# A row softmax whose loads and stores all go through one DMA queue, in one fixed order of 4 MB transfers

## Chip, cores, metric

The kernel runs on one core of one Trainium2 chip. Times are microseconds (us) on the device. The kernel before takes 162.96 us (median of 3 runs, 162.91 to 163.17). The profiled span, from first to last instruction, is about 1.8 us shorter than the time (161.2 against 162.96 us here).

## The reference, cut to what matters

```python
def reference(x):                       # x: float32, 16 x 1024 x 512
    x_scaled = x / 0.5
    x_max = np.max(x_scaled, axis=-1, keepdims=True)
    exp_x = np.exp(x_scaled - x_max)
    return exp_x / np.sum(exp_x, axis=-1, keepdims=True)
```

There are 16384 rows of 512 numbers; 33.55 MB are read and 33.55 MB written.

## The kernel before

The rows are split into 8 tiles (C = 8) of 128 partitions x 16 rows x 512, 4 MB each. A tile is worked on in four blocks of 4 rows. DVE (VectorE) takes the maximum and scales three rows of four; ACT (ScalarE) makes the exponentials with their sums and scales the fourth row. Loads are issued from Sync, stores from ACT, so two queues are at work (q1 and q10 in the profile). Six buffers of a whole tile exist.

```python
data = ctx.enter_context(tc.tile_pool(name="data", bufs=6))
...
def load(c):
    xt = tiles[c] = data.tile([P, G, D], fp32, name="xt")
    for lo, hi in FIRST if c == 0 else [(0, G)]:          # FIRST = [(0, 4), (4, 16)]
        nc.sync.dma_start(out=xt[:, lo:hi, :], in_=xr[c][:, lo:hi, :])
...
def store(i):
    c, b = blocks[i]
    if b + B == G:
        nc.scalar.dma_start(out=outr[c], in_=tiles[c])

n = len(blocks)
for i in range(n + 3):
    if i < n:
        if blocks[i][1] == 0:
            load(blocks[i][0])
        shift(i)                    # DVE: maximum, bias
        exponentials(i)             # ACT: 4 exponentials, each with its sum
    if 1 <= i <= n:
        scale_vector(i - 1)         # DVE: reciprocal, 3 scalings
    if 2 <= i <= n + 1:
        scale_scalar(i - 2)         # ACT: 1 scaling
    if 3 <= i:
        store(i - 3)
```

Of the kernel before, what the change touches and what calls it, by code (L numbers as in the profile page):

```python
# [1 line left out]

# [4 lines left out]


@with_exitstack
def kernel(  # L10
    ctx: ExitStack,
    tc: tile.TileContext,
    x: bass.AP,
    out: bass.AP,
):
    nc = tc.nc
    fp32 = mybir.dt.float32
    P = nc.NUM_PARTITIONS
    AX = mybir.AxisListType.X
    EXP = mybir.ActivationFunctionType.Exp  # L20
    COPY = mybir.ActivationFunctionType.Copy
    MAX = mybir.AluOpType.max

    D = x.shape[-1]
    xf = x.flatten_outer_dims()
    of = out.flatten_outer_dims()
    N = xf.shape[0]




    G = 16
    B = 4
    N_ACT = 1
    C = N // (P * G)
    assert C * P * G == N
    xr = xf.rearrange("(c p g) d -> c p g d", p=P, g=G)
    outr = of.rearrange("(c p g) d -> c p g d", p=P, g=G)

    FIRST = [(0, 4), (4, 16)]  # L40

    data = ctx.enter_context(tc.tile_pool(name="data", bufs=6))
    stats = ctx.enter_context(tc.tile_pool(name="stats", bufs=6))

    ctx.enter_context(tc.manual_schedule())


    warm = stats.tile([P, 1], fp32, name="warm", bufs=1)
    nc.vector.memset(warm, 0.0)  # L49
    nc.scalar.activation(out=warm, in_=warm, func=EXP)  # L50

    tiles = {}
    blocks = [(c, b) for c in range(C) for b in range(0, G, B)]
    state = {}

    def load(c):
        xt = tiles[c] = data.tile([P, G, D], fp32, name="xt")
        for lo, hi in FIRST if c == 0 else [(0, G)]:
            nc.sync.dma_start(out=xt[:, lo:hi, :], in_=xr[c][:, lo:hi, :])  # L59

    def shift(i):
        c, b = blocks[i]
        xb = tiles[c][:, b : b + B, :]
        negmax = stats.tile([P, B], fp32, name="negmax")
        nc.vector.tensor_reduce(negmax, xb, axis=AX, op=MAX, negate=True)  # L65
        bias = stats.tile([P, B], fp32, name="bias")
        nc.vector.tensor_scalar_mul(bias, negmax, 2.0)  # L67
        state[i] = (xb, bias)

    def exponentials(i):  # L70
        xb, bias = state[i]
        sums = stats.tile([P, B], fp32, name="sums")
        for g in range(B):
            nc.scalar.activation(  # L74
                out=xb[:, g, :],
                in_=xb[:, g, :],
                func=EXP,
                bias=bias[:, g : g + 1],
                scale=2.0,
                accum_out=sums[:, g : g + 1],  # L80
            )
        state[i] = (xb, sums)

    def scale_vector(i):
        xb, sums = state[i]
        recip = stats.tile([P, B], fp32, name="recip")
        nc.vector.reciprocal(recip, sums)  # L87
        for g in range(B - N_ACT):
            nc.vector.tensor_scalar_mul(xb[:, g, :], xb[:, g, :], recip[:, g : g + 1])  # L89
        state[i] = (xb, recip)  # L90

    def scale_scalar(i):
        xb, recip = state[i]
        for g in range(B - N_ACT, B):
            nc.scalar.activation(  # L95
                out=xb[:, g, :], in_=xb[:, g, :], func=COPY, scale=recip[:, g : g + 1]
            )

    def store(i):
        c, b = blocks[i]  # L100
        if b + B == G:
            nc.scalar.dma_start(out=outr[c], in_=tiles[c])

    n = len(blocks)
    for i in range(n + 3):
        if i < n:
            if blocks[i][1] == 0:
                load(blocks[i][0])
            shift(i)
            exponentials(i)  # L110
        if 1 <= i <= n:
            scale_vector(i - 1)
        if 2 <= i <= n + 1:
            scale_scalar(i - 2)
        if 3 <= i:
            store(i - 3)


# [1 line left out]
_INS = ['x']  # L120
_OUTS = [((16, 1024, 512), 'float32')]


# [23 lines left out]
```

## Time and profile before

| | before |
|---|---|
| span | 161.2 us |
| DVE, ACT busy | 74%, 71% |
| packet time in the two DMA queues, as a share of 16 engines | 49.2% + 48.2% = 97.4% |
| a 32 KB packet (packet records; median in the load, mixed and store phases) | 1213 ns |
| all bytes at that pace on 16 engines | 155.3 us |

Lines of the page of the kernel before. Part 2 has 40 slices of the span: a digit is the busy share in tenths, then come the GB/s. Part 3 has a queue's packets, MB and share of the engines' time; part 5 has a group of instructions with its busy time, the mean ns of one, and the idle time before it with what ended it; part 6 has the issues, with the median time to landing.

```profile
span 161.2 us, 563 instructions
DVE 119.7 (74%) x193; ACT 114.8 (71%) x290; POOL 0.2 (0%) x4
...
DMA  5999999998999999999999999999999999999991
GB/s 193 457 463 447 390 463 447 392 455 317 417 472 398 431 472 398 423 480 398 423 472 409 390 488 423 390 488 423 390 488 423 390 488 425 390 480 431 390 480 65
...
q1 hardware_dynamic: 1296, 33.56, 49.2%
q10 hardware_dynamic: 1152, 33.55, 48.2%
q14 instruction: 4, 0.03, 0.0%
...
L65 DVE TENSOR_REDUCE negmax<-xt 128x4 f32<-128x2048 f32 x32 | 73.0, 2281 | 19.8 <-DMA xt<-in_x_dram 19.8
...
out_dram<-xt ACTq DMA_DIRECT2D x8, 4096.0 KB, 26.9
xt<-in_x_dram SPq DMA_DIRECT2D x7, 4096.0 KB, 47.3
```

The DMA engines are busy in every slice but the first and the last. Their pace is the same in the load, mixed and store phases (1213 ns), and packets fill 97.4% of their time, so the kernel is bound by its bytes; what can still be lost lies at the start, at the end and in single slow packets. While loads and stores are mixed they share the engines evenly: from 40 to 118 us 511 packets of 32 KB start in each queue, and where the packet that follows another on its engine can be told by its start (661 cases), 587 times it is one of the other queue. The four packets of queue 14, 8 KB each, are listed as `instruction`.

Windows of the kernel before (columns: stretch, its length, busy us and count of DVE, ACT, POOL, then PEclk, DMA share, GB/s; a packet is counted where it starts):

```profile
34.00:36.00 2.00, 1.97 (x6) 1.80 (x5) 0.00 (x0) 1.00 0.74 311
36.00:38.00 2.00, 1.97 (x3) 1.75 (x6) 0.00 (x0) 1.00 1.21 360
...
158.00:159.00 1.00, 0.00 (x0) 0.00 (x0) 0.00 (x0) 1.00 0.23 98
159.00:160.00 1.00, 0.00 (x0) 0.00 (x0) 0.00 (x0) 1.00 0.00 0
```

There is a dip after the first store is issued (34.2 us): the load packets just before the first store packets, which start at 38.6 us, are slow (1.5 to 2.1 us, against 1213 ns). The last packets start before 159 us and end at 159.9 us.

### The profile page before, as it was taken

The numbers are of one execution on the slowest core, as the hardware profiler recorded it, in microseconds if no ns is written. First come the engines' busy times: TensorE is split into PE (matmuls) and PEld (weight loads), VectorE is DVE, ScalarE is ACT, GpSimd is POOL, SyncE is SP. The second block draws the span as 40 slices with busy tenths as digits, with TensorE's granted clock in tenths as the row PEclk, the third lists the DMA queues.
The fourth block names the chain that finished last, engine by engine and source line by source line (L and its number), as shares of the span: only waits on it lengthen the run. The fifth ranks groups of instructions, "written<-read, shape, count | busy, mean of one in ns | idle before, by whom it ended". The sixth has DMA issues, their size and how long they took to land.

```text
span 161.2 us, 563 instructions
## 1 busy us (share of the span) xinstructions
DVE 119.7 (74%) x193; ACT 114.8 (71%) x290; POOL 0.2 (0%) x4
## 2 busy tenths in 40 slices
DVE  0608999999999999999994999359991799930000
ACT  3072799999999998999995799809997199980000
POOL 0000000000000000000000000000000000000000
DMA  5999999998999999999999999999999999999991
GB/s 193 457 463 447 390 463 447 392 455 317 417 472 398 431 472 398 423 480 398 423 472 409 390 488 423 390 488 423 390 488 423 390 488 425 390 480 431 390 480 65
DMA packets 2452, 67.14 MB, mean 416 GB/s; under 512 B 272, under 2 KB 272, under 8 KB 272
## 3 DMA queue, kind: packets, MB, share of 16 engines
q1 hardware_dynamic: 1296, 33.56, 49.2%
q10 hardware_dynamic: 1152, 33.55, 48.2%
q14 instruction: 4, 0.03, 0.0%
HBM read 33.55 MB, written 33.55 MB: 416 GB/s over the span
## 4 chain that ended last, share of the span: by engine, by line
DMA 54%; DVE 31%; ACT 3%; issue 1%; SPq 0%
DMA xt<-in_x_dram 36%; DVE negmax L65 19%; DMA out_dram<-xt 18%; DVE xt L89 10%; ACT xt L74 2%; DVE bias L67 1%; ACT xt L95 1%; DVE recip L87 1%; SPq L59 0%
## 5 line engine op out<-in xcount | busy, mean ns | idle before, releaser
L74 ACT ACTIVATE xt<-xt,bias 128x512 f32<-128x512 f32 x128 | 90.8, 710 | 28.9 <-DVE bias L67 28.9
L65 DVE TENSOR_REDUCE negmax<-xt 128x4 f32<-128x2048 f32 x32 | 73.0, 2281 | 19.8 <-DMA xt<-in_x_dram 19.8
L89 DVE TENSOR_SCALAR xt<-xt,recip 128x512 f32<-128x512 f32 x96 | 40.9, 483 | 1.1
L74 ACT ACTIVATION_READ_ACCUMULATOR xt<-xt,bias 128x1 f32 x128 | 23.9, 187 | 0.0
L95 ACT ACTIVATE xt<-xt,recip 128x512 f32<-128x512 f32 x32 | 22.4, 706 | 0.0
L87 DVE RECIPROCAL recip<-sums 128x4 f32<-128x4 f32 x32 | 5.5, 171 | 1.6 <-ACT xt L74 1.6
L67 DVE TENSOR_SCALAR bias<-negmax 128x4 f32<-128x4 f32 x32 | 5.5, 170 | 1.1
L50 ACT ACT_TABLE_LOAD x1 | 1.3, 1283 | 0.7 <-PEq L131 0.7
L49 DVE MEMSET warm<- 128x1 f32 x1 | 0.1, 59 | 0.8 <-PEq L131 0.8
L50 ACT ACTIVATE warm<-warm 128x1 f32<-128x1 f32 x1 | 0.2, 203 | 0.0
L131 POOL MEMSET const-bfloat16-1.0<- 128x1 bf16 x1 | 0.1, 101 | 0.0
L131 POOL MEMSET const-uint8-127<- 128x1 uint8 x1 | 0.1, 101 | 0.0
L131 POOL MEMSET const-float32-0.0<- 128x1 f32 x1 | 0.1, 98 | 0.2 <-issue 0.2
L131 POOL MEMSET const-float32-1.0<- 128x1 f32 x1 | 0.1, 98 | 0.0
## 6 DMA issues: line engine op xcount, KB each, us to landing
out_dram<-xt ACTq DMA_DIRECT2D x8, 4096.0 KB, 26.9
xt<-in_x_dram SPq DMA_DIRECT2D x7, 4096.0 KB, 47.3
xt<-in_x_dram SPq DMA_DIRECT2D x1, 3072.0 KB, 11.5
xt<-in_x_dram SPq DMA_DIRECT2D x1, 1024.0 KB, 4.7
```

Of the source, the lines that this page charges most:

```text
L49: nc.vector.memset(warm, 0.0)
L50: nc.scalar.activation(out=warm, in_=warm, func=EXP)
L65: nc.vector.tensor_reduce(negmax, xb, axis=AX, op=MAX, negate=True)
L67: nc.vector.tensor_scalar_mul(bias, negmax, 2.0)
L74: nc.scalar.activation(out=xb[:, g, :], in_=xb[:, g, :], func=EXP, bias=bias[:, g : g + 1], scale=2.0, accum_out=sums[:, g : g + 1],)
L87: nc.vector.reciprocal(recip, sums)
L89: nc.vector.tensor_scalar_mul(xb[:, g, :], xb[:, g, :], recip[:, g : g + 1])
L95: nc.scalar.activation(out=xb[:, g, :], in_=xb[:, g, :], func=COPY, scale=recip[:, g : g + 1])
L131: nc = _bacc.Bacc("TRN2", target_bir_lowering=False, num_devices=1)
```

## The change

It puts all DMA into one queue with a fixed order: four tiles of loads, then a store and a load in turn. ACT issues no DMA any more, and a store stands one block earlier in the loop. The hope is an orderly stream and an ACT free of queue work.

```diff
-            nc.scalar.dma_start(out=outr[c], in_=tiles[c])
+            nc.sync.dma_start(out=outr[c], in_=tiles[c])
+            if c + 4 < C:
+                load(c + 4)
...
-    for i in range(n + 3):
+    for i in range(n + 2):
         if i < n:
-            if blocks[i][1] == 0:
-                load(blocks[i][0])
+            if i == 0:
+                for c in range(4):
+                    load(c)
...
-        if 3 <= i:
-            store(i - 3)
+        if 2 <= i <= n + 1:
+            store(i - 2)
```

With L for a tile's load and S for its store, the queue holds L0 L1 L2 L3 S0 L4 S1 L5 S2 L6 S3 L7 S4 S5 S6 S7. I call a border from a load to a store a turn: there are five, L3-S0, L4-S1, L5-S2, L6-S3 and L7-S4.

## The prediction

> **What bounds the kernel now.** Traffic. The page counts 67.14 MB, 416 GB/s over a span of 161.2 us; DVE is busy 74%, ACT 71%. Queue shares are 49.2% (loads, Sync) plus 48.2% (stores, ACT) = 97.4% of 16 engines' time. The trace's packet records say why: a 32 KB packet takes 1213 ns (median) in the pure load, the mixed and the pure store phase alike. 16 x 32768 B / 1213 ns = 432 GB/s; all bytes at that pace need 155.3 us. The first packet starts at 1.8 us, so 157.0 us is the earliest end; most packets end by 158.8, the last at 159.9. Above the ideal are about 1.8 us of packet time per engine: the first short packets (about 0.5) and some 35 slow load packets (1.5 to 2.1 us each) at 35-40 us, just after the first store (34.2 us) opens the second queue (about 1.2). The windows view shows this dip: 311 and 360 GB/s at 34-38 us. The chain of waits names DVE early (31%) only because loads run ahead.
>
> **What the change does.** No bytes or arithmetic go. By the order listing, DVE is unchanged, ACT loses 8 stores (0.34 us each of sequencer time, off the path), and Sync has 4 tiles of loads, then S0 L4 S1 L5 S2 L6 S3 L7 S4..S7. Instead of alternating by packet on each engine, loads and stores run in blocks of 4 MB, 9.7 us each. [...]
>
> **Does the one queue run dry?** A tile's compute takes 15.2 us (four blocks of 3.79); the first is ready at 34. Estimate at 9.7 us per tile: L0-L3 end at 40.6, S0 50, L4 60, S1 70, L5 79, S2 89, L6 99, S3 108, L7 118, four stores to 157. Stores are ready at 34, 49, 64, 79.5, 95, 110, 127, 139, against starts at 41, 60, 79, 99, 118, 128, 137, 147: slack at least 7 us. L6 and L7 wait for S0 and S1, which land long before. Tile 7's reduce waits some 4 us for its load, in slack. The store's earlier place in the loop gains nothing: ACT's sequencer runs ahead and already issues early stores within 0.3 us of their last scale.
>
> **Time.** Same bound, same ends (1.8 us start, about 1.3 tail, 1.75 outside the span). If the slow packets at 35-40 us come from the second queue's opening, they go: -1.2 us. The skew at the end may shrink. Against it: nine changes of direction within one queue, whose cost no trace here shows; 0.1 us each would be 0.9. Net about -0.8: 162.2 us, range 160.6 to 164.2. Floor: 157.0 + 1.3 + 1.75 = 160.0, so faster by over 2% (below 159.7) is nearly excluded. Chances: faster 0.03, same 0.92, slower 0.05.
>
> **What would show it.** Right: one queue with over 96% share, 1213 ns packets, no dip at 35-40 us, stores issued at 34, 49, 64, 79; DVE's waits for loads below the present 19.8 us; last load landing near 119 instead of 125.8 us, the end about the same. Wrong: holes in GB/s at each load-store border, or a slow stretch also with one queue (then mixing directions costs, not the second queue).
>
> **What would make it wrong.** A bubble of 0.5 us or more at each border; a limit on outstanding work in one queue that delays issues; engines drifting apart in one ring.

The sum: 162.96 - 0.8 = 162.2 us. The 0.1 us for a change of direction was assumed; as the text says, no trace showed one.

## The result

The changed kernel takes 165.16 us (165.05 to 165.25, 4 runs), against 163.06 us for the kernel before (162.91 to 163.21, 4 runs). The ratio is 1.0128 with a 95% interval of 1.0111 to 1.0146. The change costs 2.1 us, and the time lies outside the predicted range of 160.6 to 164.2.

The same lines of the page of the changed kernel:

```profile
span 163.3 us, 566 instructions
DVE 119.6 (73%) x193; ACT 114.8 (70%) x290; POOL 0.2 (0%) x4
...
DMA  5999899999799999989989999999999999999970
GB/s 183 459 466 433 385 506 393 403 490 385 323 441 401 482 401 417 474 385 449 449 385 484 409 417 466 401 433 457 393 457 433 409 474 395 433 466 393 457 321 32
...
q1 hardware_dynamic: 2448, 67.11, 96.5%
q14 instruction: 4, 0.03, 0.0%
...
L65 DVE TENSOR_REDUCE negmax<-xt 128x4 f32<-128x2048 f32 x32 | 72.9, 2279 | 17.6 <-DMA xt<-in_x_dram 17.6
...
out_dram<-xt SPq DMA_DIRECT2D x8, 4096.0 KB, 27.1
xt<-in_x_dram SPq DMA_DIRECT2D x7, 4096.0 KB, 34.3
```

The queue never ran dry, and the stores were issued when I had said. From the timeline (start, duration, queue, line, what):

```profile
34.11 0.35 SPq L102 DMA_DIRECT2D out_dram<-xt  x1
...
49.27 0.34 SPq L102 DMA_DIRECT2D out_dram<-xt  x1
...
64.43 0.34 SPq L102 DMA_DIRECT2D out_dram<-xt  x1
```

The windows of the changed kernel show two things that I had not said:

```profile
38.00:40.00 2.00, 1.97 (x6) 1.88 (x5) 0.00 (x0) 1.00 0.88 279
40.00:42.00 2.00, 1.93 (x4) 1.75 (x6) 0.00 (x0) 1.00 0.94 246
...
158.00:159.00 1.00, 0.00 (x0) 0.00 (x0) 0.00 (x0) 1.00 0.16 66
159.00:160.00 1.00, 0.00 (x0) 0.00 (x0) 0.00 (x0) 1.00 0.15 66
160.00:161.00 1.00, 0.00 (x0) 0.00 (x0) 0.00 (x0) 1.00 0.15 66
161.00:162.00 1.00, 0.00 (x0) 0.00 (x0) 0.00 (x0) 1.00 0.00 0
```

First, the dip did not go with the second queue; it moved with the first store packets and again lies just before them (the slow load packets start at 38.7 to 40.7 us, and the median engine ends these loads at 42.5 us). Second, from 158 to 161 us the DMA share is 0.15: two packets of 1213 ns over 16 engines' 1 us is 0.15. Two engines were still at work while fourteen had finished.

Why two engines are enough to set the time, the packet records show. Every transfer of these two kernels ends with 16 packets of 4 bytes (272 for 17 transfers), a transfer of one partition with a single one (late_one below: its four loads add eight packets, and four of these are under 512 B). So I take each as the end of one engine's part. The end of the changed kernel agrees: its last two 32 KB packets start at 160.60 and 160.83 us, and 1.21 us later, at 161.82 and 162.04 us, the last two 4-byte packets start; the other 14 of this store had ended by 158.9. What waited for a transfer waited for the last of its 16: tile 7's first maximum starts at 123.44 us, 0.3 us after the last one of L7 and 3.4 us after the median one (before: at 125.80, 0.4 us after the last and 2.6 us after the median). And the span ends 1.3 us after the last one of S7 in both kernels. The times of the 4-byte packets give each engine's lateness. The table has the time at which the median engine ended a transfer, and how far the last two engines were behind it (us, worked out from the packet records of the two profiles). While the two queues of the kernel before are mixed, lateness in one queue is not the lateness of the engine (in few_two below it is 1.7 us in the load queue at L3 and 0.3 us in the store queue at S0); the rows S7 can be compared.

```
changed kernel                              before, load queue
transfer  median   2nd last  last           transfer  median   2nd last  last
L2         31.57   0.14      0.57           L2         31.45   0.21      0.26
L3         42.48   0.20      1.47           L3         45.77   0.69      1.87
S0         52.16   0.86      1.47
L4         61.89   1.38      2.32           L4         65.13   0.69      1.87
S1         71.57   1.39      2.32
L5         81.25   1.86      2.32           L5         84.52   1.37      2.17
S2         90.93   1.86      2.76
L6        100.66   2.63      3.07           L6        103.88   1.49      2.17
S3        110.34   2.63      3.07
L7        120.02   2.63      3.07           L7        123.24   1.49      2.17
                                            before, store queue
S7        158.82   3.00      3.22           S7        158.34   1.49      1.60
```

So the 2.1 us are accounted for: the median engine ends 0.5 us later (158.82 against 158.34), and the last engine is 1.6 us further behind it (3.22 against 1.60).

The table also shows when it happens. The instruction packets of the changed kernel start at 31.8, 43.9, 88.4 and 134.8 us, last 309 ns each, and are followed by a gap or slow packet on the engine that carried one; an engine falls 0.4 to 0.7 us behind by one. Those are the steps at L2 (0.57), S0 (0.86), S2 (2.76) and after L7. All other steps, 0.3 to 0.9 us each, stand at L3, L4, L5 and L6: at the turns. None stands at S1 or S3, where a store is followed by a load, and none at L7, the fifth turn. For one of the two engines the sum is 1.3 us by two fetches and 1.8 us by turns; for the other 0.9 and 2.1. The slow packet at one of these turns is among the late engine's last three of the load (at L4 one of them runs from 60.90 to 63.01 us). It begins between 1.5 us before and 0.2 us after the median engine ends its loads, and runs on while others store.

Theory A, then: an engine that has been put out of step, first by an instruction fetch, loses more at the turns of a one-queue order in large blocks; with loads and stores mixed by packet it does so less. Rivals: B, one queue for both directions costs by itself; C, two engines are slow by their place; D, fetches cost only their own bytes, and turns add nothing.

### The profile page after: what moved, and what is told of

It reads as the page before. It is cut to its first block, busy times and chain, and to the rows that moved or that the text cites. A ratio compares the mean times of both kernels' runs of the same rounds, so it can differ in the third digit from the quotient of the medians.

```text
span 163.3 us, 566 instructions
## 1 busy us (share of the span) xinstructions
DVE 119.6 (73%) x193; ACT 114.8 (70%) x290; POOL 0.2 (0%) x4
## 3 DMA queue, kind: packets, MB, share of 16 engines
q1 hardware_dynamic: 2448, 67.11, 96.5%
## 4 chain that ended last, share of the span: by engine, by line
DVE 47%; DMA 34%; ACT 5%; issue 1%; SPq 0%; ACTq 0%
DMA xt<-in_x_dram 34%; DVE negmax L65 28%; DVE xt L89 15%; ACT xt L74 4%; DVE bias L67 2%; ACT xt L95 1%; DVE recip L87 1%; ACTq L145 0%; SPq L59 0%; SPq L102 0%
## 5 line engine op out<-in xcount | busy, mean ns | idle before, releaser
L65 DVE TENSOR_REDUCE negmax<-xt 128x4 f32<-128x2048 f32 x32 | 72.9, 2279 | 17.6 <-DMA xt<-in_x_dram 17.6
```

The source lines that it names most:

```text
L65: nc.vector.tensor_reduce(negmax, xb, axis=AX, op=MAX, negate=True)
```

## The experiments

Experiments with wrong numbers move the same bytes in the same transfers. Lateness is always the last engine's end behind the median engine's, in the profiled run, so it stands for one execution of each kernel. Every ratio is to the kernel before in the same rounds.

### Fewer turns: six_ahead, pairs

six_ahead loads six tiles ahead, then a store and a load in turn (`range(4)` and `c + 4` become `range(6)` and `c + 6`). pairs does

```diff
-                for c in range(4):
+                for c in range(6):
                     load(c)
...
-            if c + 4 < C:
-                load(c + 4)
+            if c == 1:
+                load(6)
+                load(7)
```

> The changed kernel with six tiles of loads ahead in its one queue instead of four: the turns from loads to stores fall from four (L3-S0, L4-S1, L5-S2, L6-S3, L7-S4 are five with the last) to three. Theory A (two of the 16 DMA engines fall behind, first by an instruction fetch, then more at each turn from loads to stores): the two late engines end 2.0 to 2.7 us after the median engine, not 3.0 to 3.2, and the span is 162.3 to 162.9 us against 163.3. Rival B (one queue for both directions costs by itself, wherever the turns are): lag and span as in the changed kernel, 163.3 within 0.2.

> One queue, six tiles ahead, then two stores, two loads, six stores: only two turns from loads to stores. Theory A: late engines end 1.6 to 2.2 us after the median, span 161.6 to 162.4 us. Rival B: span 163.3 within 0.2.

six_ahead: 170.59 us (ratio 1.0448), a mistake of mine. There are six buffers, so L6 waits until S0 has landed, and Sync holds S1 behind that wait (L6 and L7 waited for stores for 61.2 us in all): the queue ran dry, and later once more (3.2 and 2.0 us of idle time per engine in the packet records). Its windows:

```profile
70.00:72.00 2.00, 2.00 (x1) 2.00 (x6) 0.00 (x0) 1.00 0.42 180
72.00:74.00 2.00, 1.93 (x7) 1.75 (x6) 0.00 (x0) 1.00 0.00 0
...
104.00:106.00 2.00, 2.00 (x2) 2.00 (x7) 0.00 (x0) 1.00 1.30 524
106.00:108.00 2.00, 1.93 (x7) 1.75 (x6) 0.00 (x0) 1.00 1.09 262
```

It does not test the number of turns, but it showed two things. After a dry stretch the engines are in step again (lateness 1.71 before, 0.30 after). And the next turn after it costs every engine about 1 us again (1.0 us of excess packet time per engine around 83 us, 1.1 around 106), like the first turn of each run, while the second to fifth turns of the changed kernel cost the median engine nothing.

pairs: 163.79 us (ratio 1.0035, 1.0010 to 1.0059), span 162.2, lateness 2.16. Same queue, same bytes, four instruction packets as in the changed kernel, right numbers, two turns in place of five, and 1.4 us faster than the changed kernel. This lies in theory A's range and outside B's.

### More turns: halves

```diff
-            nc.sync.dma_start(out=outr[c], in_=tiles[c])
-            if c + 4 < C:
-                load(c + 4)
+            ...
+            for lo in (0, G // 2):     # store and load half a tile in turn
+                nc.sync.dma_start(out=outr[c][:, lo:hi, :], in_=tiles[c][:, lo:hi, :])
+                if c + 4 < C:
+                    nc.sync.dma_start(out=xt[:, lo:hi, :], in_=xr[c + 4][:, lo:hi, :])
```

> The changed kernel with stores and loads alternating by half tiles (2 MB, packets of 16 KB): nine turns from loads to stores instead of five, same bytes. Theory A: late engines end 4 us or more after the median, span 164.3 or more. Rival B: span 163.3 within 0.3. If packets of 16 KB cost something themselves, the median engine ends later too, which would be read apart.

166.32 us (ratio 1.0187), span 164.0. The median engine ended 0.5 us later than in the changed kernel (159.32), but the lateness was 3.31, not 4 or more. Theory A in its simple form, so much for each turn, fails here: turns closer together, with packets of 16 KB, cost less each (3.31 us after nine of them, 3.22 after five in the changed kernel). The lateness seems to be bounded.

### Without fetches, and one engine late on purpose: few_one, quiet_one, late_one

few_one uses one activation for a block and one scaling on DVE in place of three, and drops the bias product (wrong numbers); quiet_one also makes blocks of 8 rows (the first load is cut at 8 rows too), scales on DVE alone and stores as soon as a tile is done. The queue's order stays.

```diff
-        for g in range(B):
-            nc.scalar.activation(out=xb[:, g, :], in_=xb[:, g, :], func=EXP,
-                bias=bias[:, g : g + 1], scale=2.0, accum_out=sums[:, g : g + 1])
+        nc.scalar.activation(out=xb, in_=xb, func=EXP,
+            bias=bias[:, 0:1], scale=1.0, accum_out=sums)
```

late_one is quiet_one plus, after the first block's exponentials,

```diff
+                for k in range(4):     # [1, 2047]: one engine, 8 KB; never read
+                    nc.scalar.dma_start(out=late[k : k + 1, 0:2047], in_=...)
```

> The changed kernel's queue and order, with one activation per block instead of four, one scaling instead of three, and no bias product: wrong numbers on purpose, same bytes, so few instructions that none should have to be fetched in the run. Theory A: no instruction packets inside the run, no engine out of step, the last engine ends within 0.6 us of the median, span 159.9 to 160.6 us. Rival C (two engines are slow by their place, whatever is fetched): they still end 2 us or more after the median, span 162 or more. Rival B: span 163 or more.

> The one queue in the order of the changed kernel, with blocks of 8 rows, one instruction each for maximum, exponential and scaling (wrong numbers on purpose, same bytes and the same transfers): so few instructions that nothing should be fetched before the last stores. Theory A (an engine put out of step by a fetch loses more at each turn from loads to stores): without a fetch no engine lags over 0.6 us at the end, last store's median engine at 158.8, span 159.9 to 160.7 us. Rival C (two engines slow by their place): a lag of 1.5 us or more remains, span over 161.3.

> The one-queue kernel with few instructions, plus four loads of one partition (8 KB each, one engine) into an unused tile in the first microseconds, which put one engine some 1.3 us out of step before the first turn. Theory A: this one engine loses more at the turns, ends 2.2 us or more behind the median, and the span is 161.6 us or more. Rival D (only the fetched bytes delay, turns add nothing): it ends 1.2 to 1.5 us behind, span about 161.1.

few_one: 163.18 us, runs from 162.59 to 163.27 (ratio 0.9989). The fetches were halved, not gone (`q14 instruction: 2` on its page, at 63 and 68 us); lateness 1.48, span 161.5. That is half way, in theory A's direction, outside its range; B's and C's numbers for the lateness or the span did not come either.

quiet_one: 162.96 us (ratio 0.9980), span 160.9, no instruction packet in the run. Lateness 1.18, above the 0.6 that I had expected, but no fetch was needed for it: one engine 0.3 us behind after the first turn grew to 0.44, 0.77 and 1.18 at L5, L6 and L7.

late_one: 165.08 us (ratio 1.0112), span 163.2. Four loads, 33 KB out of 67 MB, on one engine, cost 2.1 us against quiet_one. Windows of quiet_one, then of late_one:

```profile
157.00:158.00 1.00, 0.00 (x0) 0.00 (x0) 0.00 (x0) 1.00 1.14 492
158.00:159.00 1.00, 0.00 (x0) 0.00 (x0) 0.00 (x0) 1.00 0.08 33
159.00:160.00 1.00, 0.00 (x0) 0.00 (x0) 0.00 (x0) 1.00 0.00 0
```

```profile
158.00:159.00 1.00, 0.00 (x0) 0.00 (x0) 0.00 (x0) 1.00 0.08 33
159.00:160.00 1.00, 0.00 (x0) 0.00 (x0) 0.00 (x0) 1.00 0.08 33
160.00:161.00 1.00, 0.00 (x0) 0.00 (x0) 0.00 (x0) 1.00 0.08 33
161.00:162.00 1.00, 0.00 (x0) 0.00 (x0) 0.00 (x0) 1.00 0.00 0
```

A share of 0.08 is one packet of 1213 ns in 16 us: one engine alone. Its lateness, from the packet records:

```
            L2    L3    S0    L4    S1    L5    S2    L6    S3    L7    S7
quiet_one  0.19  0.30  0.30  0.35  0.35  0.44  0.44  0.77  0.77  1.18  1.18
late_one   1.08  1.89  1.90  2.73  2.73  2.73  2.73  3.14  3.14  3.40  3.40
later_one  2.40  3.24  3.24  3.24  3.24  3.24  3.24  3.80  3.80  3.80  3.80
```

After L2 every step of late_one stands at a load that precedes a store. Rival D is out: the engine was given 1.08 us of lateness and lost 2.3 us more. Rival C is out as the whole cause, because this engine was chosen by me; but in quiet_one an engine lost 1.0 us that was given nothing, and why it was that engine no run shows.

### Two queues with few instructions: quiet_two, late_two, few_two

The same reductions in the kernel before.

> The two queues of the kernel before, with the same few instructions (wrong numbers on purpose). Theory A: no fetch, so the late engines of the kernel before (1.5 to 1.6 us behind the median at its end) go too: lag under 0.6 us, span 159.4 to 160.2 us; the difference between one queue and two shrinks from 2.1 us to under 0.7. Rival C: lag and difference stay.

> The same four one-engine loads in the two-queue kernel with few instructions. Theory A: loads and stores mix by packet and there is only one turn, so the engine ends 1.2 to 1.7 us behind the median, and the one-queue kernel with the same loads ends at least 0.7 us later than this one. Rival D: both end equally late within 0.5 us.

> The kernel before, two queues, with one activation, one scaling and no bias product for each block of four rows (wrong numbers on purpose), so half the instruction fetches. Theory A: the last engine, 1.6 us behind the median in the kernel before, is at most 1.0 us behind, span 160.2 to 160.9 us. If an engine falls far behind in the mixed phase as in quiet_two, span over 162, and then mixing by packet is not safe by itself.

quiet_two: 169.44 us (ratio 1.0379). With nothing fetched, one engine fell behind all the same, by 1.5 us at L3 and 8.8 us at L6 in the load queue (6.4 us at S3 in the store queue), all during the mixed phase; tiles then came so late that the stores ran dry at about 139 us. late_two: 164.68, 164.69, 168.01 and 171.08 us, two of them over 1.5% above the fastest; in the profiled run (164.68) the last store was issued only at 149.4 us, and the queue had run dry. Blocks of 8 rows make the last tile too late for two queues, where its load lands after 128 us. Neither run can be compared with its one-queue partner. But quiet_two shows that mixing by packet is no protection by itself; why that engine went on losing while those of the kernel before kept their lateness for 19 us of mixing (1.87 in the load queue at L3 and at L4) stays open.

few_two (blocks of 4 rows, few instructions): 162.03 us (ratio 0.9927, 0.9911 to 0.9944), span 160.3, lateness 0.74, as theory A said. The median engine ended its last store at 158.34 us, as in the kernel before, so the gain lies in the lateness: the kernel before, too, seems to carry its fetches to the end. The fewer instructions also move the first store forward, which this run does not part from the fetches.

### More fetches: pool_one, pool_two

```diff
+    for _ in range(512):
+        nc.gpsimd.memset(busy[0:1, :], 0.0)       # GpSimd is idle otherwise
```

> The changed kernel, right numbers, plus 512 one-element memsets on the otherwise idle GpSimd, which touch nothing of the work but whose instructions have to be fetched, some four times 8 KB, most of it before the first turn. Theory A: the engine that carries GpSimd's fetches is put some 2 us or more out of step before the first turn, loses more at the turns, ends 4 us or more behind the median; span 164.3 us or more against 163.3. Rival D (fetches only cost their own bytes, the turns cost the two known engines by their place): the third engine ends at most 2.7 us behind, span stays at 163.3 within 0.3.

> The same idle memsets in the kernel before, two queues. Theory A as first stated (one turn only, then mixing): the lateness stays near the fetched amount, 2 to 3 us behind the median at the end, span 161.4 to 162.8 us, so that the one-queue kernel with memsets is at least 1.8 us slower than this one. But the run with two queues and few instructions had one engine fall 8 us behind in the mixed phase: if being out of step costs there as well, this span is over 163.

pool_one: 165.18 us (ratio 1.0115), span 163.5. Eight fetches instead of four; three engines late in place of two, by 2.29, 2.90 and 3.53 us. The third late engine came with the added fetches. But I had expected 4 us or more and a span of 164.3; the lateness stayed below 3.6, and the span is the one that D had. pool_two: 163.88 us (ratio 1.0036), span 162.0 and lateness 2.51, as said. The two differ by 1.3 us and not by 1.8. The direction holds, and again the lateness in one queue is bounded.

### Is the dip the first store's or the turn's: early_two, early_one

```diff
+            if c == 0 and lo == 0:      # 64 KB of zeros, overwritten later by S0
+                nc.sync.dma_start(out=outr[0][:, 0, 0:128], in_=first)    # scalar in early_two
```

> The kernel before, plus a store of 64 KB of zeros to rows that the first tile's store overwrites later, issued with the first loads. If the slow load packets at 35 to 40 us (about 1 us on every engine) are a cost of the very first store of a run, they go, and the span falls by 0.6 to 1.0 us to about 160.4. If they belong to the turn of full-rate loads to stores (the run with six tiles ahead showed about 1 us at each turn that followed a dry queue), nothing goes: 161.0 to 161.6.

> The same early store in the changed kernel's one queue, between the first two loads. First-store theory: the slow packets at 38 to 42 us go, span 162.1 to 162.7 us. Turn theory: they stay, span 163.1 to 163.7.

early_two: 163.12 us (ratio 0.9990), span 161.6. early_one: 165.45 us (ratio 1.0118), span 163.7. The excess packet time at the turn fell from 1.0 to 0.6 us per engine and from 1.2 to 0.8, but did not go, and neither span fell. The dip belongs mostly to the turn, and six_ahead says the same.

### Does the queue or the order cost: mix_one, mix_cols

Both keep the one queue and alternate small pieces in it; mix_one by 16 partitions, mix_cols by two rows of all 128 partitions.

```diff
+                for lo in range(0, G, 2):                     # mix_cols
+                    hi = lo + 2
+                    nc.sync.dma_start(out=outr[c][:, lo:hi, :], in_=tiles[c][:, lo:hi, :])
+                    nc.sync.dma_start(out=xt[:, lo:hi, :], in_=xr[c + 4][:, lo:hi, :])
```

> The changed kernel with its one queue, but stores and loads of the mixed part cut into pieces of 16 partitions (one packet for each engine) and issued in turn, so that loads and stores alternate by packet as with two queues, right numbers. If the blocks of 4 MB cost (theory A), the last engine ends at most 2.2 us behind the median, near the 1.6 of the kernel before, and the two late engines do not jump at 60, 80 and 100 us. If one queue costs (rival B), the lag stays at 3 us or more. Small transfers may move the median engine later by themselves (about 0.04 us for each extra transfer in the run with halves, so up to 2 us), hence the verdict is on the lag behind the median, not on the time.

> The changed kernel, right numbers, with stores and loads of the mixed part cut into pieces of two rows of all 128 partitions (0.5 MB, 1.2 us of each engine) and issued in turn in the one queue. Theory A: as with two queues, no jumps of the late engines at 60, 80 and 100 us, last engine at most 2.2 us behind the median. Rival B: 3 us or more behind. The many transfers may move the median itself by up to 2 us; the verdict is on the lag. If alternating in one queue is slow by itself, the packets will be over their pace (1213 ns for 32 KB), as in mix_one.

mix_one failed as an experiment: 205 to 251 us, four runs that do not agree. In the profiled one (250.53 us) a 32 KB packet took 2.57 us on average in the mixed part (80 to 200 us) instead of 1.21. It says nothing of queue or order.

mix_cols: 165.47 us (ratio 1.0139), right numbers. Its packets of 4 KB took 159 ns against 152 at the pace of 32 KB packets, and the median engine ended at 160.67 us, 1.9 us later than in the changed kernel. The lateness is 1.73 us at the end, about that of the kernel before (1.60), and from 42 to 120 us the last engine's value never grew: 1.03 at the first piece, 1.00 at the last but one. Only with the last piece of load, where the pure stores begin and an instruction packet falls (121.6 us), it rose by 0.7. It had five instruction packets where the changed kernel has four. Its windows at the times of the former turns:

```profile
60.00:62.00 2.00, 1.93 (x6) 1.75 (x5) 0.00 (x0) 1.00 1.03 420
80.00:82.00 2.00, 2.00 (x4) 2.00 (x7) 0.00 (x0) 1.00 1.03 422
100.00:102.00 2.00, 2.00 (x2) 2.00 (x7) 0.00 (x0) 1.00 1.02 416
```

One queue with a fine mix did not build up the lateness (1.03 us to 1.00); one queue with blocks of 2 or 4 MB did (3.31 us in halves, 3.22 in the changed kernel). Rival B is out as far as the lateness goes. That mix_cols is not faster is the price of its small transfers: in its mixed part the median engine took 1.25 us for each 0.5 MB piece instead of 1.21. It changes the packet size (4 KB for 32 KB) along with the mix, and no run parts these two.

### How the loss depends on turns and lateness: late_pairs, later_one

late_pairs is late_one in the order of pairs; later_one has eight one-engine loads for four.

> The kernel with few instructions and one engine put late on purpose (wrong numbers on purpose), in the order of six tiles of loads, two stores, two loads, six stores: two turns where the run late_one had five. Theory A: that engine starts from 1.1 us, gains 0.7 to 0.9 at each of two turns and ends 2.4 to 2.9 us behind, not 3.4, with the span 0.5 to 1.0 us below the 163.2 of late_one. Rival B: 3.4 and 163.2.

> As late_one with eight one-engine loads instead of four, so some 2.2 us late before the first turn. If the loss at a turn does not depend on the lateness, it gains 2.3 us as there and ends 4.3 to 4.8 us behind; if it grows with it, 5.2 or more; if the lateness is bounded near what all runs showed (3.2 to 3.5), under 4.

late_pairs: 164.09 us (ratio 1.0047), span 161.9. The late engine gained 0.8 us at the first turn and nothing at the second, and ended 2.07 us behind, not 3.40. Fewer turns cost less, even less than I had said.

later_one: 165.41 us (ratio 1.0132), span 163.6. The engine was 2.40 us late at L2, with its eighth load still to come, and 3.80 at the end (third line of the table above): it started at least 1.3 us later than in late_one, and the kernel took 0.3 us longer. A second engine, 0.43 us late at L2, lost 1.2 us more at the first turn and ended 2.45 us behind; the run does not say why. In no one-queue run with blocks of 2 or 4 MB that did not run dry did the last engine end more than 3.8 us behind, and this is why halves and pool_one stayed under my numbers. What sets that bound, and what makes a load slow while other engines store, no run shows.

## Why the prediction was wrong, point by point

- "Same bound": right. The 32 KB packet stayed at 1213 ns (median), the queue's share was 96.5%, and it never ran dry.
- Stores "ready at 34, 49, 64, 79.5": right, issued at 34.1, 49.3, 64.4 and 79.6. DVE's waits for loads fell from 19.8 to 17.6 us, as said, and brought nothing, because DVE is not the bound.
- Last load "landing near 119": the median engine ended it at 120.0, the last one 3.1 us later, and tile 7's first maximum started at 123.4.
- "If the slow packets at 35-40 us come from the second queue's opening, they go: -1.2 us": wrong. They came at the first turn in one queue as well, as long as before or longer (1.2 us per engine against 1.0). The prediction had named this as a sign that mixing directions costs, and not the second queue.
- "The skew at the end may shrink": this is the step that failed. It doubled, from 1.6 to 3.2 us, and it decides the time, because the kernel ends with the last of 16 engines (1.3 us after its last packet in both).
- "nine changes of direction within one queue [...] 0.1 us each would be 0.9": wrong in kind. Changes from store to load cost nothing that shows (after S0 the median engine of the changed kernel ends a transfer every 9.68 to 9.73 us, and eight packets of 1213 ns are 9.70), the first from load to store costs every engine about 1 us, in both kernels, the next three cost one or both of the two late engines 0.3 to 0.9 us each and the median engine nothing, and the fifth cost nothing. I took one average where engines must be looked at one by one.
- "engines drifting apart in one ring" stood among the things that would make it wrong, with no number. The four instruction packets stood on the page before; I had not asked what one costs the engine that carries it (0.4 to 0.7 us).

As a sum: predicted were 162.2 us, measured 165.16, so 3.0 us are missing. My net of -0.8 was -1.2 for the slow packets, +0.9 for the borders and, as what is left, since the text gives it no number, about -0.5 for the skew. In their place stand +1.6 for the lateness and +0.5 for the median engine, whose slow packets stayed: +2.1 instead of -0.8 makes 2.9. The kernel before was 0.1 us slower beside the changed one than in its first runs.

No version with right numbers beat the kernel before. few_two, whose numbers are wrong, shows what is to be had with half of the fetches and fewer instructions (1.1 us), but with right numbers ACT runs one instruction and one read-out of its sum for each of a partition's 128 rows here (710 and 187 ns, x128 each, on the page before), and I found no way to halve that.

## What to carry to other kernels

In a kernel bound by DMA bytes, look at the sixteen engines one by one at the end of the run: here the last decided, and a share of 0.08 or 0.15 in the last microseconds of the windows was one or two stragglers. The pace does not show them: a 32 KB packet took 1213 ns with one queue and with two, and yet the one queue in blocks of 4 MB cost 1.3% of the time without running dry. An order in large blocks of one direction in one queue let an engine that was out of step fall further behind at turns from loads to stores, up to 3.8 us in these runs, so an orderly stream can be worse than a fine mix (165.16 against 163.06 us). A mix by packet is not safe by itself either (quiet_two). Look at the instruction packets too: one of 8 KB, 309 ns long, left its engine 0.4 to 0.7 us behind (changed kernel), though a lateness of 1.2 us came without any (quiet_one). And a load that reuses the buffer of the store just ahead of it in the same queue drained that queue, with 3.2 and 2.0 us of idle DMA engines here (six_ahead).
